# Modulation by two passes with four stationary columns in a one-core hybrid diffusion layer

## Chip, cores and metric

The kernel runs on one core of a Trainium2 chip. The metric is the device time of one execution in microseconds. Before the change three runs took 1698.61, 1699.95 and 1700.68 us; their median is 1699.95 us.

## What is computed

One layer of a diffusion backbone on 1024 latent tokens and 256 context tokens of width 1024. Only its first step matters here: two conditioning vectors, `c` and `c_ctx`, go through silu and a projection, and the first two sixths of the result (shift and scale) modulate the normalised tokens in front of the input projection:

```python
sh1, sc1, gt1, sh2, sc2, gt2 = jnp.split((jax.nn.silu(c) @ w_mod + b_mod)[:, None, :], 6, axis=-1)
sh1c, sc1c, ... = jnp.split(jax.nn.silu(c_ctx) @ w_mod + b_mod, 6, axis=-1)
p = modulate(x, norm1_g, sh1, sc1) @ w_in        # rms_norm(x, g) * (1 + scale) + shift
pc = modulate(xc, norm1_g, sh1c, sc1c) @ w_in
...
```

What follows (differential attention, a gated DeltaNet in both directions, the output projection, sixteen experts chosen by the experts, a final norm) is not touched. All values are float32, w_mod is 1024 x 6144.

## The kernel before

Products of float32 values are made from rounded parts. `K.split(hi, lo, src)` (L174) rounds `src` to fp32r on ACT (L175) and takes the rest, `src - hi`, on DVE or, where it is given, on POOL (L176). `K.mm3` (L167) then multiplies in three passes: high by high (L170), low by high (L171), high by low (L172).

`_modulation` (L525) is the first stage. The small vectors come by seven DMAs into `vr`, 110 rows of 128; PE transposes them (L546), DVE copies them to `vec` (L547). From `vec` come `convw` (L549), half of the two conditioning vectors `xh` (L553), their tanh on ACT (L554) and silu, `cs` (L555). `cs` is split into `csh` and `csl` (L558), for each of eight k-tiles two columns, one for `c` and one for `c_ctx`. These are the stationary operands.

The moving operand is w_mod, columns 0 to 2047, in eight k-tiles `wm` of 128 x 2048 (1 MB each, L532, SP's queue, three buffers). Each k-tile is taken in four parts j of 512 columns: split into `wmh` and `wml` (four buffers each, `WMB`), then multiplied into `pmod`, two rows of PSUM (L574). Of the rests, the one of j = 3 is made on POOL for k-tiles 0 to 5, the others on DVE. In the last k-tile the parts j = 2, 3 are multiplied unsplit, as exact fp32 products (L570). Afterwards the two rows are copied out of PSUM (L581 on ACT, L582 on DVE), turned by sixteen transposes of 2 x 128 (L585), and biases are added (L586, L588): `modA` and `modB`.

Beside this stage the kernel loads the first context tokens and w_in's columns for the values. `K.after` (L115) has POOL write one element of a buffer, so that its load cannot start before a given step. `_tokens` (L593) squares (L603), normalises (L606 to L612) and transposes tokens (L617), and modulates them (L621 to L623); the latent tokens' loads wait for `mod`. `_inproj` (L368) follows: projections of ten token tiles, then of heads. For the rotary heads (L439) halves of the head are exchanged by eight DMAs a half-head from ACT's queue (L449), multiplied on POOL (L452) and written out (L458, L459).

No order is written out by hand. The planner of the tile framework (`schedule_with_timeline_sim=True`, L1743) orders every engine's and every DMA queue's instructions by planned times; of those ready at a time, those of higher priority go first, and `tc.high_priority(n)` raises the priority of what is written under it. On the chip each queue runs strictly in that order, and instructions wait for one another by semaphores.

Of the kernel before, what the change touches and what calls it, by code (L numbers as in the profile page):

```python
# [18 lines left out]
F32 = mybir.dt.float32  # L19
F32R = mybir.dt.float32r  # L20
BF16 = mybir.dt.bfloat16
I32 = mybir.dt.int32
AF = mybir.ActivationFunctionType
ALU = mybir.AluOpType
# [4 lines left out]
P = 128  # L29
D = 1024  # L30
KT = D // P
# [41 lines left out]
QP, WP = (3,), (1, 3, 5)  # L73
# [294 lines left out]
def _inproj(K, banks):  # L368
# [8 lines left out]
    with tc.tile_pool(name="p1v", bufs=1, reuse_waits="tile") as pv, \  # L377
# [3 lines left out]
        with tc.tile_pool(name="p0", bufs=1, reuse_waits="tile") as pe:  # L381
            with tc.tile_pool(name="p0m", bufs=1, space=PSUM, side="right", reuse_waits="tile") as psm:
                xts, *late, raws = _modulation(K, pe, ps0, psm)
            for j in range(4):
                if j < 2:
                    wr = pv.tile([P, 2, 528], F32, name="wvr", bufs=2)
                    K.after(wr[:, 0, 0:1], late[0])
                else:
                    wr = raws.pop(0)[:, :2 * 528].rearrange("p (k f) -> p k f", k=2)
                nc.sync.dma_start(wr[:, :, 0:512], w_in[:, 2 * j:2 * j + 2, 1024:1536])  # L390
                nc.sync.dma_start(wr[:, :, 512:528], w_in[:, 2 * j:2 * j + 2, 3584:3600])
                for i in range(2):
                    K.split(wvh[:, 2 * j + i], wvl[:, 2 * j + i], wr[:, i], nc.gpsimd if 2 * j + i in WP else None)
            K.after(K.cstt[:, 0:1], late[1])
            nc.sync.dma_start(K.cstt, a["cst"][:, P:])
            _tokens(K, pe, ps0, xts, late)
# [119 lines left out]
def _load_tokens(K, pe, t, after=None):  # L516
    xt = pe.tile([P, D], F32, name="xt", bufs=6)
    if after is not None:
        K.after(xt[:, 0:1], after)
    src = K.a["x"][0, t * P:(t + 1) * P] if t < NT else K.a["ctx"][0, (t - NT) * P:(t - NT + 1) * P]  # L520
    K.nc.sync.dma_start(xt, src)
    return xt


def _modulation(K, pe, ps, psm):  # L525

    tc, nc, a = K.tc, K.nc, K.a
    ident = K.cst(C_IDENT)

    def load(kt):  # L530
        wm = pe.tile([P, 2048], F32, name="wm", bufs=3)
        nc.sync.dma_start(wm, a["w_mod"][0, kt * P:(kt + 1) * P, 0:2048])  # L532
        return wm

    vr = pe.tile([110, P], F32, name="vr")
    rows = (a["c"].rearrange("b (k p) -> (b k) p", p=P), a["c_ctx"].rearrange("(k p) -> k p", p=P),
            a["b_mod"].rearrange("l (k p) -> (l k) p", p=P), a["norm1_g"].rearrange("l (k p) -> (l k) p", p=P),
            a["conv_w"].rearrange("l i (k p) -> (l i k) p", p=P), a["gdn_norm_g"], a["da_subln_g"])
    r = 0
    for i, src in enumerate(rows):  # L540
        if i == AT:
            first = load(0)
        (nc.scalar if i % 2 else nc.sync).dma_start(vr[r:r + src.shape[0]], src)
        r += src.shape[0]
    pv = ps.tile([P, 512], F32, name="pv", tag="px", bufs=3)[:, :110]
    nc.tensor.transpose(pv, vr, ident[:110, :110])  # L546
    nc.vector.tensor_copy(K.vec, pv)  # L547
    vec = K.vec
    nc.vector.tensor_scalar(K.convw, vec[:, 72:109], 0.5, None, op0=ALU.mult)  # L549

    xh = pe.tile([P, 16], F32, name="xh")
    th = pe.tile([P, 16], F32, name="th")
    nc.vector.tensor_scalar(xh, vec[:, 0:16], 0.5, None, op0=ALU.mult)  # L553
    nc.scalar.activation(th, xh, AF.Tanh)  # L554
    nc.vector.scalar_tensor_tensor(K.cs, th, 1.0, xh, op0=ALU.add, op1=ALU.mult)  # L555
    csk = K.cs.rearrange("p (w k) -> p k w", w=2)
    csh, csl = (pe.tile([P, KT, 2], F32R, name=nm) for nm in ("csh", "csl"))
    K.split(csh, csl, csk)  # L558
    pm = psm.tile([2, 2048], F32, name="pmod")
    xts, los = {}, []  # L560
    for kt in range(KT):
        wm = load(kt) if kt else first
        if kt in XKT:
            t = TOKENS[XKT.index(kt)]
            xts[t] = _load_tokens(K, pe, t, los[kt - 3])

        for j in (2, 3, 0, 1) if kt == KT - 1 else range(4):
            js = slice(j * 512, (j + 1) * 512)
            if j > 1 and kt == KT - 1:
                nc.tensor.matmul(pm[:, js], csk[:, kt], wm[:, js], start=False, stop=True)  # L570
                continue
            hi, lo = (pe.tile([P, 512], F32R, name=nm, bufs=WMB) for nm in ("wmh", "wml"))
            K.split(hi, lo, wm[:, js], nc.gpsimd if j in QP and kt < 6 else None)
            K.mm3(pm[:, js], csh[:, kt], csl[:, kt], hi, lo, kt == 0, kt == KT - 1)  # L574
        los.append(lo.bitcast(F32)[:, 0:1])
    raws = [pe.tile([P, 2048], F32, name="wvr", tag="wm", bufs=3) for _ in range(2)]
    mrow = pe.tile([P, 2048], F32, name="mrow", tag="wm", bufs=3)[:2]
    mod = pe.tile([P, 8, 2], F32, name="mod")
    with tc.high_priority():
        for i in (1, 0):  # L580
            nc.scalar.activation(mrow[:, i * D:i * D + 512], pm[:, i * D:i * D + 512], AF.Copy)  # L581
            nc.vector.tensor_copy(mrow[:, i * D + 512:(i + 1) * D], pm[:, i * D + 512:(i + 1) * D])  # L582
            pmt = ps.tile([P, 512], F32, name="pmt", tag="px", bufs=3)[:, :16]
            for j in range(8):
                nc.tensor.transpose(pmt[:, 2 * j:2 * j + 2], mrow[:, i * D + j * P:i * D + (j + 1) * P], ident[:2, :2])  # L585
            nc.vector.tensor_tensor(mod if i else K.modB, pmt.rearrange("p (k w) -> p k w", w=2),  # L586
                                    vec[:, 16 + 8 * i:24 + 8 * i].unsqueeze(2).to_broadcast([P, 8, 2]), ALU.add)
        nc.vector.scalar_tensor_tensor(K.modA, mod, 1.0, vec[:, 64:72].unsqueeze(2).to_broadcast([P, 8, 2]),  # L588
                                       op0=ALU.add, op1=ALU.mult)
    return xts, los[LATE[0]], mod[:, 0, 0:1], raws  # L590
# [1156 lines left out]
```

## Time and profile before

| | us |
|---|---|
| median of three runs | 1699.95 |
| the profiled execution | 1699.86 |
| its span, first to last instruction | 1698.1 |
| PE busy | 1540.2 |
| DVE busy | 1301.8 |
| ACT busy | 908.1 |
| POOL busy | 614.3 |

The profiled execution lies 0.09 us under the median, and 1.76 us of it lie around the span. PE, DVE, ACT and POOL are TensorE, VectorE, ScalarE and GpSimd; SP issues DMAs. The busy times are averages over stages of different kinds: the stage that the change touches is the first 42 us or so. In a timeline, a line gives the start, the time taken, the engine, the line of the kernel and the tiles; consecutive instructions of one kind are drawn together (x4), and what stands in brackets is the engine's idle time just before and what ended it. A matmul's duration is longer than its distance from the next one, since they are pipelined.

### The profile page before, as it was taken

The page shows a single profiled execution, that of the slowest core. Times are in us where ns is not written, and L with a number is a line of the kernel's source. Part 1 is how long each engine was busy: PE and PEld are TensorE (multiplying, and loading weights), DVE is VectorE, ACT ScalarE, POOL GpSimd, SP SyncE. Part 2 cuts the span into 40 slices and gives each one's busy share as a digit, 9 for nine tenths or more (in the row PEclk, how much of TensorE's full clock was granted, in tenths as well). Part 3 has the DMA queues.
Part 4 walks back from the last instruction along what each step waited for, and adds up shares of the span by engine and source line. Part 5 has one row for each costly group of instructions (what it writes and reads, how often), then busy time and mean ns, then how long its engine had stood idle before and what let it go on. Part 6 is the DMA issues. An engine that isn't in the chain of part 4 may idle for free.

```text
span 1698.1 us, 24820 instructions
## 1 busy us (share of the span) xinstructions
PE 1540.2 (91%) x8782; PEld 1301.7 (77%) x8782; DVE 1301.8 (77%) x2111; ACT 908.1 (53%) x1508; POOL 614.3 (36%) x554
## 2 busy tenths in 40 slices
PE   6999889899988999999898898399999999999994
PEld 2897668788867988888888787278888887778882
DVE  6657654586768877778787644799999998899986
ACT  6521125344423655656565232288777776777772
POOL 3013331322236774482720122435355433342101
PEclk9999999999997999999999999599999999999997
DMA  7477943444556042413122584699999999999965
GB/s 271 164 246 223 282 137 118 142 124 130 181 162 173 20 111 78 120 64 108 58 86 86 159 294 169 243 361 343 403 396 395 379 397 377 355 387 386 363 245 185
DMA packets 171280, 378.76 MB, mean 223 GB/s; under 512 B 32590, under 2 KB 82188, under 8 KB 170004
## 3 DMA queue, kind: packets, MB, share of 16 engines
q1 hardware_dynamic: 131874, 315.22, 51.2%
q0 software_dynamic: 12096, 45.09, 8.9%
q10 hardware_dynamic: 27186, 16.86, 3.8%
q8 instruction: 69, 1.13, 0.3%
q14 instruction: 55, 0.45, 0.1%
HBM read 316.65 MB, written 56.29 MB: 220 GB/s over the span
## 4 chain that ended last, share of the span: by engine, by line
PE 54%; DVE 14%; DMA 7%; POOL 3%; issue 3%; ACT 3%; SPq 1%; ACTq 0%; POOLq 0%; DVEq 0%
PE pgu L170 4%; PE pgu L172 3%; PE pgu L171 3%; PE pgv L172 3%; PE pgv L170 3%; PE pgv L171 3%; PE py L170 3%; PE py L171 3%; PE py L172 3%; PE po L1066 2%; DMA qe<-eg_dram 2%; PE sp L1038 2%; PE pp L170 2%; PE pp L171 2%; PE sp L1039 2%
## 5 line engine op out<-in xcount | busy, mean ns | idle before, releaser
L1478 DVE TENSOR_TENSOR wlo<-raw,whi 128x1024 fp32r<-128x1024 f32 x368 | 439.4, 1238 | 29.7 <-ACT whi L1477 10.0
L1477 ACT ACTIVATE whi<-raw 128x1024 fp32r<-128x1024 f32 x376 | 390.8, 1060 | 102.5 <-PE pgu L171 36.4
L1425 POOL TENSOR_SCALAR onehot<-fcst,slot 128x128 bf16<-128x128 f32 x96 | 142.0, 1493 | 156.9 <-PE pls L1428 156.9
L171 PE MATMUL pl<-XH,wl 128*128 128x512 f32 x384 | 152.8, 398 | 3.6 <-DVE wl L176 3.6
L170 PE MATMUL pl<-XH,wh 128*128 128x512 f32 x384 | 153.1, 399 | 0.9 <-DVE ab L411 0.9
L172 PE MATMUL pl<-XL,wh 128*128 128x512 f32 x384 | 153.4, 399 | 0.0
L1044 ACT ACTIVATE pt<-sp,mx 128x1280 f32<-128x1280 f32 x64 | 84.9, 1326 | 56.7 <-DVE mx L1041 56.1
L1041 DVE TENSOR_REDUCE mx<-sp 128x1 f32<-128x1280 f32 x64 | 95.0, 1485 | 22.1 <-PE sp L1039 22.0
L170 PE MATMUL pgu<-whi,xTh 128*128 128x512 f32 x256 | 102.2, 399 | 5.0 <-ACT xTh L175 4.2
L172 PE MATMUL pgu<-wlo,xTh 128*128 128x512 f32 x256 | 101.7, 397 | 0.0
L172 PE MATMUL pgv<-wlo,xTh 128*128 128x512 f32 x256 | 101.2, 395 | 0.0
L171 PE MATMUL pgu<-whi,xTl 128*128 128x512 f32 x256 | 100.9, 394 | 0.0
L170 PE MATMUL pgv<-whi,xTh 128*128 128x512 f32 x256 | 100.6, 393 | 0.0
L171 PE MATMUL pgv<-whi,xTl 128*128 128x512 f32 x256 | 100.2, 391 | 0.0
L170 PE MATMUL py<-whi,hTh 128*128 128x512 f32 x240 | 94.6, 394 | 2.0 <-DVE y L1542 2.0
L172 PE MATMUL py<-wlo,hTh 128*128 128x512 f32 x240 | 94.6, 394 | 0.9 <-DVE wlo L1478 0.9
L171 PE MATMUL py<-whi,hTl 128*128 128x512 f32 x240 | 95.0, 396 | 0.0
L170 PEld LDWEIGHTS pl<-XH,wh 128*128 128x128 f32 x384 | 73.4, 191 | 20.4 <-issue 5.2
L171 PEld LDWEIGHTS pl<-XH,wl 128*128 128x128 f32 x384 | 73.2, 191 | 20.1 <-DVE wl L176 3.9
L1066 PE MATMUL po<-V,aT 128*128 128x128 f32 x640 | 87.8, 275 | 0.0
L1038 PE MATMUL sp<-KH,QS 128*128 128x512 f32 (+1 forms) x192 | 77.0, 401 | 9.9 <-ACT pt L1044 5.7
L172 PEld LDWEIGHTS pl<-XL,wh 128*128 128x128 f32 x384 | 73.2, 191 | 15.4 <-issue 0.9
(560 smaller groups left out, 3995.9 us busy)
## 6 DMA issues: line engine op xcount, KB each, us to landing
raw<-w_gate SPq DMA_DIRECT2D x64, 1024.0 KB
raw<-w_up SPq DMA_DIRECT2D x64, 1024.0 KB
raw<-w_down SPq DMA_DIRECT2D x64, 1024.0 KB
rwm<-w_mod POOLq DMA_DIRECT2D x32, 512.0 KB, 6.3
wr<-w_in ACTq DMA_DIRECT2D x24, 512.0 KB
wm<-w_mod SPq DMA_DIRECT2D x8, 1024.0 KB
KH<-qk_dram SPq DMA_DIRECT2D x16, 320.0 KB
xt<-x SPq DMA_DIRECT2D x8, 512.0 KB
```

The source lines that it names most:

```text
L170: nc.tensor.matmul(out, ah, bh, start=start, stop=False)
L171: nc.tensor.matmul(out, al, bh, start=False, stop=False)
L172: nc.tensor.matmul(out, ah, bl, start=False, stop=stop)
L1038: nc.tensor.matmul(sp[:, k0:k1], qs, st["KH"][s][:, k0:k1], start=True, stop=False)
L1039: nc.tensor.matmul(sp[:, k0:k1], padded[t % 2][:, s], st["KL"][:, k0:k1], start=False, stop=True)
L1041: nc.vector.tensor_reduce(mx, sp[:, :LT], axis=AX.X, op=ALU.max, negate=True)
L1044: nc.scalar.activation(pt, sp[:, :LT], AF.Exp, bias=mx, accum_out=sm)
L1066: nc.tensor.matmul(po, aT[c], st["V"][:, c], start=c == 0, stop=c == NTT - 1)
L1425: eng.tensor_scalar(oh[:, t], iota, slot[:, t, e:e + 1], None, op0=ALU.is_equal)
L1477: nc.scalar.activation(hi, raw[:, i], AF.Copy)
L1478: eng.tensor_tensor(lo, raw[:, i], hi.bitcast(F32), ALU.subtract)
```

## The change

- The rounded parts and the rests of silu lie side by side in one tile `cs4`: for each k-tile four columns, rounded `c`, rounded `c_ctx`, rest of `c`, rest of `c_ctx`. One pass with `wmh` and one with `wml` as the moving operand give four rows of PSUM; the product of the two rests comes in as well. The three-pass `mm3` is not used here any more.
- The four rows are summed while they are turned: instead of a transpose, a product with `both`, a 4 x 2 tile with ones where row and row + 2 are to be added.
- The chain from `vr` to `cs4` stands under a priority of 5000, and `convw` behind it.
- For j = 0, 1 of the first k-tile the rounding goes from ACT to POOL (a copy), and the rest is made on DVE as before.

```diff
@@ -542,21 +542,25 @@
-    pv = ps.tile([P, 512], F32, name="pv", tag="px", bufs=3)[:, :110]
-    nc.tensor.transpose(pv, vr, ident[:110, :110])
-    nc.vector.tensor_copy(K.vec, pv)
     vec = K.vec
-    nc.vector.tensor_scalar(K.convw, vec[:, 72:109], 0.5, None, op0=ALU.mult)
 
     xh = pe.tile([P, 16], F32, name="xh")
     th = pe.tile([P, 16], F32, name="th")
-    nc.vector.tensor_scalar(xh, vec[:, 0:16], 0.5, None, op0=ALU.mult)
-    nc.scalar.activation(th, xh, AF.Tanh)
-    nc.vector.scalar_tensor_tensor(K.cs, th, 1.0, xh, op0=ALU.add, op1=ALU.mult)
     csk = K.cs.rearrange("p (w k) -> p k w", w=2)
-    csh, csl = (pe.tile([P, KT, 2], F32R, name=nm) for nm in ("csh", "csl"))
-    K.split(csh, csl, csk)
-    pm = psm.tile([2, 2048], F32, name="pmod")
+    cs4 = pe.tile([P, KT, 4], F32R, name="cs4")
+    with tc.high_priority(5000):
+        pv = ps.tile([P, 512], F32, name="pv", tag="px", bufs=3)[:, :110]
+        nc.tensor.transpose(pv, vr, ident[:110, :110])
+        nc.vector.tensor_copy(vec, pv)
+        nc.vector.tensor_scalar(xh, vec[:, 0:16], 0.5, None, op0=ALU.mult)
+        nc.scalar.activation(th, xh, AF.Tanh)
+        nc.vector.scalar_tensor_tensor(K.cs, th, 1.0, xh, op0=ALU.add, op1=ALU.mult)
+        K.split(cs4[:, :, 0:2], cs4[:, :, 2:4], csk)
+    nc.vector.tensor_scalar(K.convw, vec[:, 72:109], 0.5, None, op0=ALU.mult)
+
+    both = pe.tile([4, 2], F32, name="both")
+    nc.vector.tensor_tensor(both, ident[:4, 0:2], ident[:4, 2:4], ALU.add)
+    pm = psm.tile([4, 2048], F32, name="pmod")
     xts, los = {}, []
     for kt in range(KT):
@@ -567,14 +571,20 @@
         for j in (2, 3, 0, 1) if kt == KT - 1 else range(4):
             js = slice(j * 512, (j + 1) * 512)
             if j > 1 and kt == KT - 1:
-                nc.tensor.matmul(pm[:, js], csk[:, kt], wm[:, js], start=False, stop=True)
+                nc.tensor.matmul(pm[:2, js], csk[:, kt], wm[:, js], start=False, stop=True)
                 continue
             hi, lo = (pe.tile([P, 512], F32R, name=nm, bufs=WMB) for nm in ("wmh", "wml"))
-            K.split(hi, lo, wm[:, js], nc.gpsimd if j in QP and kt < 6 else None)
-            K.mm3(pm[:, js], csh[:, kt], csl[:, kt], hi, lo, kt == 0, kt == KT - 1)
+            if not kt and j < 2:
+
+                nc.gpsimd.tensor_copy(hi, wm[:, js])
+                nc.vector.tensor_tensor(lo, wm[:, js], hi.bitcast(F32), ALU.subtract)
+            else:
+                K.split(hi, lo, wm[:, js], nc.gpsimd if j in QP and kt < 6 else None)
+            nc.tensor.matmul(pm[:, js], cs4[:, kt], hi, start=kt == 0, stop=False)
+            nc.tensor.matmul(pm[:, js], cs4[:, kt], lo, start=False, stop=kt == KT - 1)
         los.append(lo.bitcast(F32)[:, 0:1])
     raws = [pe.tile([P, 2048], F32, name="wvr", tag="wm", bufs=3) for _ in range(2)]
-    mrow = pe.tile([P, 2048], F32, name="mrow", tag="wm", bufs=3)[:2]
+    mrow = pe.tile([P, 2048], F32, name="mrow", tag="wm", bufs=3)[:4]
     mod = pe.tile([P, 8, 2], F32, name="mod")
@@ -582,7 +592,7 @@
             for j in range(8):
-                nc.tensor.transpose(pmt[:, 2 * j:2 * j + 2], mrow[:, i * D + j * P:i * D + (j + 1) * P], ident[:2, :2])
+                nc.tensor.matmul(pmt[:, 2 * j:2 * j + 2], mrow[:, i * D + j * P:i * D + (j + 1) * P], both, start=True, stop=True)
```

## Rows read from the trace of the kernel before

**Rows 1.** Page, part 2: PE's busy tenths in 40 slices.
```profile
PE   6999889899988999999898898399999999999994
```

**Rows 2.** Windows: us, busy us (x instructions) by engine, PEclk, DMA share, GB/s.
```profile
16.30:19.70 3.40, 3.40 (x17) 1.23 (x15) 2.68 (x4) 3.27 (x7) 1.83 (x2) 1.00 0.30 53
19.70:33.90 14.20, 11.62 (x49) 3.31 (x47) 11.81 (x22) 11.57 (x21) 6.76 (x6) 1.00 1.00 396
33.90:42.30 8.40, 7.46 (x39) 2.86 (x37) 8.30 (x13) 5.91 (x11) 4.25 (x5) 1.00 0.37 93
42.30:49.40 7.10, 5.52 (x25) 4.66 (x24) 4.66 (x10) 3.76 (x7) 2.23 (x5) 0.52 0.98 354
...
25.00:30.00 5.00, 3.29 (x13) 0.76 (x11) 4.66 (x13) 3.17 (x7) 2.98 (x3) 1.00 0.99 380
```

**Rows 3.** Timeline of ACT, 0 to 46 us: start, us, what, [idle before <-releaser].
```profile
6.83 2.19 ACT L175 ACTIVATE wmh<-wm 128x512 fp32r<-128x512 f32 x4 [3.17 <-DMA wm<-w_mod]
...
10.74 0.22 ACT L175 ACTIVATE csh<-cs 128x16 fp32r<-128x16 f32 x1 [1.61 <-DVE cs L555]
13.40 0.63 ACT L175 ACTIVATE wmh<-wm 128x512 fp32r<-128x512 f32 x1 [2.44 <-PE pmod L171]
...
26.53 2.19 ACT L175 ACTIVATE wmh<-wm 128x512 fp32r<-128x512 f32 x4 [0.55 <-PE pmod L172]
30.12 2.19 ACT L612 ACTIVATE xt<-xt,nt 128x1024 f32<-128x1024 f32 x2 [1.40 <-DVE nt L163]
...
36.43 1.13 ACT L175 ACTIVATE wmh<-wm 128x512 fp32r<-128x512 f32 x2
```

**Rows 4.** Timeline of PE, 10 to 16 us.
```profile
11.01 1.87 PE L170 MATMUL pmod<-wmh,csh 128*2 128x512 f32 x4 [3.74 <-ACT csh L175]
12.68 0.63 PE L171 MATMUL pmod<-wmh,csl 128*2 128x512 f32 x1
...
15.24 0.40 PE L171 MATMUL pmod<-wmh,csl 128*2 128x512 f32 x1
15.48 0.40 PE L172 MATMUL pmod<-wml,csh 128*2 128x512 f32 x1
```

**Rows 5.** Timeline of SP's queue: the issue of k-tile 4.
```profile
17.83 0.33 SPq L532 DMA_DIRECT2D wm<-w_mod  x1
```

**Rows 6.** Timeline of DVE, 0 to 46 us.
```profile
7.31 0.27 DVE L547 COPY vec<-pv 128x110 f32<-128x110 f32 x1 [7.31 <-PE pv L546]
7.50 0.69 DVE L176 TENSOR_TENSOR wml<-wm,wmh 128x512 fp32r<-128x512 f32 x1
...
8.20 0.17 DVE L553 TENSOR_SCALAR xh<-vec 128x16 f32<-128x16 f32 x1
...
9.48 1.23 DVE L555 SCALAR_TENSOR_TENSOR cs<-th,xh 128x16 f32<-128x16 f32 x1
...
42.92 0.55 DVE L622 TENSOR_SCALAR xm<-px,modA,modB 128x256 f32<-128x256 f32 x1 [0.63 <-ACT XH L621]
```

**Rows 7.** Timeline of POOL, 0 to 46 us.
```profile
9.11 1.57 POOL L176 TENSOR_TENSOR wml<-wm,wmh 128x512 fp32r<-128x512 f32 x1 [8.68 <-ACT wmh L175]
...
42.56 1.31 POOL L176 TENSOR_TENSOR wvl<-wvr,wvh 128x528 fp32r<-128x528 f32 x1
```

**Rows 8.** Groups of POOL, by form: the copy nearest in size.
```profile
L343 POOL COPY fb<-cst 80x512 f32<-80x512 f32 x4 | 2.5, 614 | 0.0
```

**Rows 9.** Timeline of PE from 35 us: the exact products, the result's transposes.
```profile
35.81 1.88 PE L570 MATMUL pmod<-wm,cs 128*2 128x512 f32 x4
...
40.70 0.66 PE L585 MATMUL pmt<-ident,mrow 2*128 2x2 f32 x8
...
41.65 0.40 PE L585 MATMUL pmt<-ident,mrow 2*128 2x2 f32 x4
```

**Rows 10.** Chain that ended last, 200 to 260 us: start, us, what.
```profile
246.00 0.61 ACTq L449
...
249.49 3.28 POOL rxs L452
```

## Prediction, written before the changed kernel was run

> **What bounds the kernel now.** I read the page's slices first, then the windows of the first 60 us, then each engine's timeline there. After its first slice TensorE (PE) is busy in tenths of 8 and 9 through most of the run [rows 1], so a microsecond saved in front, while PE still waits for the modulation, should arrive at the end. The change touches nothing behind about 42.3 us directly; what it can save is looked for ahead of that.
>
> There the windows show three things [rows 2]. DMA, the source of the eight 1 MB k-tiles of w_mod, is saturated from 19.70 to 33.90 us (share 1.00, 396 GB/s), but in the 3.40 us before that it stands almost still (0.30, 53 GB/s). In the last 8.40 us the DVE is the engine that is full (8.30 us). PE is not full in 19.70 to 33.90 (11.62 of 14.20 us): its count of passes is not in itself the limit.
>
> The hole in the DMA has a cause that can be followed back. There are three buffers for k-tiles; k-tile 4 is issued at 17.83 us [rows 5], once every part of k-tile 1 has been split. ACT began to split k-tile 1 only at 13.40 us, after 2.44 us of waiting for PE's pass L171 [rows 3]: the four buffers of rounded parts were still being read. And PE began only at 11.01 us, when ACT had made csh [rows 3, 4]. So the bound is a latency: vector chain, then PE, then ACT, then the DMA's ring.
>
> **Start of PE.** Removed from the path to csh: convw, and DVE and ACT work planned ahead of the chain (ACT does four splits from 6.83 us for 2.19 us, two of which go to POOL). Without any hold: vec ends at 7.58; five short steps (xh 0.17, then tanh, cs, rounded part 0.22 and rest at the same 0.17 to 0.22) make 0.95 us, and hand-overs with ACT, which is busy until 6.83 + 2.19/2 = 7.9 us with its two remaining splits, some 0.3 us more: 8.8 us [rows 3, 6]. That is the early end.
>
> But two copies are added on POOL at just this time. Near copies took 0.61 us each [rows 8]. The row of cs shows what they can do: 1.23 us for 16 columns, when xh took 0.17; it ends at 10.71, just after POOL's subtraction ended at 9.11 + 1.57 = 10.68 [rows 6, 7]. The DVE stood still for POOL. An operation that reads PSUM was not held: xm took 0.55 us inside POOL's 1.31 us [rows 6, 7]; so vec should pass, xh may not. I take one hold by a copy, 0.61 us, and one subtraction wml put between, 0.69 us [rows 6]: PE starts at 8.8 + 1.3 = 10.1 us. Late end: cs is held by POOL's subtraction again, 1.23 - 0.17 = 1.06 us more: 11.2 us.
>
> The Trainium skill (SBUF — State Buffer, Who interferes with whom) speaks against this part: the engine that issues first keeps the pair of ports shared by VectorE and GpSimd for its whole instruction, and the other blocks. By that rule xh, cs and the rest could each be held in turn, and the sum would come out at its late end, a gain of under 1 us. The cs row agrees; whether all three are held no row here shows.
>
> **Two passes instead of three.** 30 products lose a pass: 90 passes become 60. At the spacing after 15.24 us, 0.24 us (the spacing before it was (12.68 - 11.01)/4 = 0.42 us) [rows 4], that is 7.2 us of PE work. I cost most of this at nothing: in 19.70 to 33.90 us DMA, ACT and DVE cover it [rows 2]. What counts is the first k-tile. Before, the buffer of j=0 became free only when the pass with csl had read it, 13.40 - 11.01 = 2.39 us behind PE's start. Now one product with four columns reads it: from the start of that last reading pass to ACT's next split it was 13.40 - 12.68 = 0.72 us [rows 3, 4]. So k-tile 1 begins at 10.1 + 0.72 = 10.8 us instead of 13.40: **2.6 us earlier** (bounds: 8.8 + 0.72 = 9.5, or 3.9 earlier; 11.2 + 0.72 = 11.9, or 1.5 earlier). The pace after that is unchanged until PE is at its full clock: two passes a product then as now.
>
> **How it carries.** k-tile 4 is issued 2.6 us earlier, at 15.2 us; the hole shrinks from 3.4 to 0.8 us, and all later landings move by 2.6 us. One further wait of ACT for PE, 0.55 us at 26.53, should go too, since a k-tile now has 8 passes in place of 12 [rows 3]. The DVE's work in the last 8.4 us is unchanged, so it moves along. Together 3.1 us (3.9 + 0.55 = 4.5 at most, 1.5 at least).
>
> **What is added.** The last transposes become full fp32 products with `both`. Two exact fp32 products left four records of PE, while 8 transposes left 8 records in 0.66 us and 4 in 0.40 us [rows 9]; so the added products leave twice the records, at (0.66 - 0.40)/4 = 0.065 us each. The last four cost 0.26 us on the path, the eight before them up to 0.52 us more; they wait for the copies out of PSUM, so I take 0.5 in all (0.26 to 0.78). The tile `both` is made from ident while DVE waits for its first operand until 7.31 us [rows 6]: nothing; without that cover one short step, 0.17 us. The copies of four rows instead of two have the same columns: nothing. The two copies on POOL delay its subtraction of k-tile 0 by nothing where ACT's fourth split ended at 6.83 + 2.19 = 9.02, since two copies end at 8.1; with that cover gone they delay the ring's next issue by at most 1.2 us, about what separates the late start from the one I take. cs4 takes the room of csh and csl. No DMA is added.
>
> **The sum** is 3.1 - 0.5 = 2.6 us off the profiled execution's 1699.86 us (span 1698.1 and 1.76 around it; the median of the runs is 1699.95, the same to 0.1): **1697.3 us**. Bounds: 4.5 - 0.26 = 4.2 and 1.5 - 0.78 = 0.7 us gained, 1695.7 to 1699.2. A measurement of this kernel can tell about 0.2%, 3.4 us, from no change.
>
> **Rivals.** *More than the latency.* If nothing holds the chain (3.9) and ACT's 1.40 us wait at 30.12 for the context tokens' norm [rows 3] also goes with a less crowded DVE: 3.9 + 0.55 + 1.40 - 0.5 = 5.3 us, 1694.5. For it: ACT and DVE have such idle spots all along. Against: DVE is at 11.81 of 14.20 us and DMA at 1.00 [rows 2], and neither has less to do. In 42.30 to 49.40 us the clock was granted at 0.52 on average [rows 2], near the 1.2 GHz level; if the shift lets PE run that stretch at 2.4 GHz, its 5.52 busy us shrink by up to 2 us: 1692.5.
>
> *The chain is not ahead.* If POOL's copies and subtraction hold it as before, PE starts at 11.2 us, and only the earlier release is left: 1.5 - 0.5 = 1 us, 1699.
>
> *PE falls to half its clock.* With a third fewer passes PE has gaps between k-tiles. At 0.42 us a pass, 60 passes from 10.1 us end at 35.3, the exact products at twice 1.88 us at 39.1; the transposes begin then rather than at 40.70, and take 1.0 us more: 0.6 us gained, 1699.3, no change. Against it: in 25 to 30 us PE was busy 3.29 of 5 us and the clock stayed at 1.00 [rows 2], and 8 passes at 0.24 us in the 2.65 us that 1.05 MB takes at 396 GB/s are about the same share. The Trainium skill (TensorE: Matmul & The Clock Gate, HAM oscillation — how this bites in real kernels) warns of this pattern, bursts of matmuls between waits for the next tile; by that rule this rival would be the likeliest, and the 25 to 30 us row disagrees.
>
> *Slower: another plan for a queue far behind.* All queues are ordered by a planner from planned times, which move as well. The stage at 200 to 260 us is on the chain that ended last through ACT's queue of rope exchanges, 0.61 us an issue, eight for a half-head, and then POOL's product of 3.28 us [rows 10]. If the new plan puts one half-head's issues in front of those that are waited for, that is 8 x 0.61 + 3.28 = 8.2 us; less 2.6, slower by 5.6: 1705.5. It decides from 2.6 us of added wait on; one burst without the product is +2.3, 1702.2. For it: these queues run in order, and each issue is long. Against: a uniform shift leaves the order as it is.
>
> **Chances.** Forecast 0.42, of which 0.12 beyond 3.4 us (bound 4.2); more than the latency 0.30; not ahead 0.06; half clock 0.06; slower plan 0.16. Faster by over 0.2%: 0.12 + 0.30 = 0.42. Within: 0.30 + 0.06 + 0.06 = 0.42. Slower: 0.16. The range goes from the clock's 1692.5 to one burst with the late start, 1699.86 - 0.7 + 4.9 = 1704.
>
> **What would show it.** Right: PE's first product near 10.1 us, ACT's split of k-tile 1 near 10.8, the issue of k-tile 4 near 15.2, a hole in the DMA of under 1.5 us, no wait of ACT for PE behind 20 us, the first XH near 39.7 us, and the same offset at 240 us and at the end. Wrong: PE's start at or behind 11 us with xh, cs or the rest drawn out beside a POOL copy; a granted clock of 0.5 between 16 and 38 us; or an offset at 240 us unlike that at 40 us, which would be the planner's.

## The result, and the profile after

The changed kernel took 1706.68 us (median of 8 runs, 1704.40 to 1712.49), the kernel before, in the same session, 1698.26 us (8 runs, 1691.96 to 1701.89). The ratio is 1.0058, 95% interval 1.0040 to 1.0075: the change makes it slower by 0.6%, where 2.6 us less had been forecast. The profiled execution took 1704.40 us, its span is 1702.6 us, so again 1.8 us lie around it.

The chain that the prediction followed did what it said. On PE, ACT and SP, in timelines of the changed kernel (from the copies of `mrow` on, line numbers are ten above those of before):

```profile
9.85 0.59 PE L583 MATMUL pmod<-wmh,cs 128*4 128x512 f32 x1 [2.41 <-DVE cs L176]
...
26.59 0.40 PE L584 MATMUL pmod<-wml,cs 128*4 128x512 f32 x1 [1.40 <-DVE wml L176]
...
28.34 0.39 PE L584 MATMUL pmod<-wml,cs 128*4 128x512 f32 x1 [1.12 <-DVE wml L176]
...
38.34 0.40 PE L584 MATMUL pmod<-wml,cs 128*4 128x512 f32 x1
39.41 2.84 PE L595 MATMUL pmt<-both,mrow 4*128 4x2 f32 x24 [0.68 <-ACT mrow L591]
...
42.55 1.48 PE L595 MATMUL pmt<-both,mrow 4*128 4x2 f32 x8
```

```profile
10.47 0.63 ACT L175 ACTIVATE wmh<-wm 128x512 fp32r<-128x512 f32 x1 [0.98 <-PE pmod L583]
...
24.10 2.20 ACT L175 ACTIVATE wmh<-wm 128x512 fp32r<-128x512 f32 x4 [0.51 <-DMA wm<-w_mod]
28.39 2.19 ACT L622 ACTIVATE xt<-xt,nt 128x1024 f32<-128x1024 f32 x2 [2.09 <-DVE nt L163]
...
38.77 0.59 ACT L591 ACTIVATE mrow<-pmod 4x512 f32<-4x512 f32 x1 [2.94 <-PE pmod L584]
40.10 0.59 ACT L591 ACTIVATE mrow<-pmod 4x512 f32<-4x512 f32 x1 [0.74 <-DVE mrow L592]
...
45.37 1.48 ACT L631 ACTIVATE XH<-px,modB,modA 128x256 fp32r<-128x256 f32 x3 [1.85 <-DVE modB L596]
```

```profile
15.25 0.33 SPq L532 DMA_DIRECT2D wm<-w_mod  x1
...
24.32 0.45 SPq L532 DMA_DIRECT2D wm<-w_mod  x1
```

Of the kernel before, the last k-tile's issue, the last product into `pmod`, the last add of the modulation and the first XH:

```profile
27.37 0.34 SPq L532 DMA_DIRECT2D wm<-w_mod  x1
...
40.16 0.39 PE L172 MATMUL pmod<-wml,csh 128*2 128x512 f32 x1
...
42.12 0.17 DVE L586 TENSOR_TENSOR modB<-pmt,vec 128x16 f32<-128x16 f32 x1
...
42.32 0.56 ACT L621 ACTIVATE XH<-px,modB,modA 128x256 fp32r<-128x256 f32 x1 [0.43 <-DVE modB L586]
```

Against these and [rows 3 to 5]: PE starts at 9.85 us instead of 11.01, ACT splits k-tile 1 at 10.47 instead of 13.40, k-tile 4 is issued at 15.25 instead of 17.83. The last k-tile's issue moved from 27.37 to 24.32 us, 3.05 earlier. But at 28.39 us, where ACT normalises the context tokens, the lead is 1.73 us (30.12 in [rows 3]); at the last product into `pmod` it is still 1.8 (38.34 + 0.40 = 38.74, against 40.16 + 0.39 = 40.55). From there on everything is later: XH starts at 45.37 us instead of 42.32.

These are single executions, and some of these times scatter. Two more profiles of the front of before (e17 and e3 below) end the last product at 39.27 and 41.59 us, two more of the changed front (e1 and e2) at 38.48 and 38.60. Over three profiles each, the mean lead is 3.4 us at the last issue and 1.9 us at the last product. What follows the last product does not scatter: from its end to the start of `modB` it is 1.56 or 1.57 us in all three profiles of the old front and 6.44 or 6.45 us in all three of the new one. DVE, and POOL's one row, show this end in detail:

```profile
7.87 1.29 DVE L559 TENSOR_SCALAR convw<-vec 128x37 f32<-128x37 f32 x1
9.08 0.16 DVE L557 SCALAR_TENSOR_TENSOR cs<-th,xh 128x16 f32<-128x16 f32 x1
...
39.39 0.68 DVE L592 COPY mrow<-pmod 4x512 f32<-4x512 f32 x1 [1.11 <-ACT mrow L591]
40.72 0.68 DVE L592 COPY mrow<-pmod 4x512 f32<-4x512 f32 x1 [0.65 <-ACT mrow L591]
...
43.03 2.23 DVE L176 TENSOR_TENSOR wvl<-wvr,wvh 128x528 fp32r<-128x528 f32 x2 [0.61 <-ACT wvh L175]
45.18 0.16 DVE L596 TENSOR_TENSOR modB<-pmt,vec 128x16 f32<-128x16 f32 x1
```

```profile
7.86 1.26 POOL L176 TENSOR_TENSOR wml<-wm,wmh 128x512 fp32r<-128x512 f32 x1
```

Three things stand between 38.74 and 45.18 us. The four copies out of `pmod` go one behind the other, each waiting for the one before on the other engine (39.39, 40.10 and 40.72 us). The products with `both` follow at (2.84 - 0.25)/23 = 0.11 us a record, two records a product; the last eight, where the clock falls, take 1.48. And when they are done, at 42.55 + 1.48 = 44.03 us, DVE is not free: the planner has put two splits of the next matrix ahead of `modB`, 43.03 to 45.2 us.

The first two of these rows of DVE belong together with POOL's. `convw` takes 1.29 us where it took 0.18 before, beside POOL's subtraction, and `cs`, whose tanh is ready at 8.21 us, starts only behind it, at 9.08. In e1, the same kernel once more, `convw` starts 0.02 us ahead of POOL's subtraction (7.88 to 9.16 us) instead of 0.01 us behind it; it takes 0.18 us, and `cs` itself is drawn out, to nearly the same end:

```profile
7.86 0.18 DVE L559 TENSOR_SCALAR convw<-vec 128x37 f32<-128x37 f32 x1
8.23 0.95 DVE L557 SCALAR_TENSOR_TENSOR cs<-th,xh 128x16 f32<-128x16 f32 x1 [0.20 <-ACT th L556]
```

The windows, as in [rows 2], and PE's slices, as in [rows 1]:

```profile
16.30:19.70 3.40, 3.04 (x13) 0.74 (x12) 2.96 (x5) 3.40 (x8) 1.29 (x1) 1.00 1.01 416
19.70:33.90 14.20, 9.31 (x27) 1.60 (x26) 10.37 (x23) 11.30 (x20) 5.39 (x6) 0.84 0.85 329
33.90:42.30 8.40, 7.72 (x36) 3.56 (x35) 6.55 (x9) 4.17 (x8) 3.90 (x4) 0.86 0.48 132
42.30:49.40 7.10, 6.35 (x29) 5.17 (x30) 4.98 (x10) 3.75 (x8) 2.44 (x6) 0.55 0.91 334
```

```profile
PE   6999889899977999999998898299999999999994
```

The hole in the DMA is gone (share 1.01 instead of 0.30). The granted clock is 0.84 and 0.86 from 19.70 to 42.30 us, where it was 1.00: it stays at 1.00 until 29.2 us and is 0.58 from there to 37.3 us, behind two waits of PE for DVE (1.40 us at 26.59, 1.12 us at 28.34). In the slices PE falls from 8 to 7 in the twelfth and thirteenth, 468 to 553 us.

Far behind, at 520 to 1000 us, the views differ too. What the change touches ends at 45 us, but the planner put other instructions first there on all engines; from some 80 to 520 us and behind 1000 us the order is nearly the same. PE's waits from 520 to 1000 us (total us, times, longest), of the kernel before and of the changed one:

```profile
PE sp L1038 <- ACT pt L1044: 5.7, 8, 1.9
```

```profile
PE sp L1048 <- ACT pt L1054: 11.1, 9, 2.9
PE pot L1092 <- DVE aO L1089: 6.8, 2, 6.5
```

The wait for `aO`, one of 6.5 us, is not there before. The same wait stands in all four profiles that have the new order behind 520 us (this one and, of the runs below, e1, e3 and e16) and in none of the fifteen with the old one.

### The profile page after: what moved, and what is told of

It is laid out like the page before. It is cut to its first block, busy times and chain, and to the rows that moved or that the text cites. A ratio compares the mean times of both kernels' runs of the same rounds, so it can differ in the third digit from the quotient of the medians.

```text
span 1702.6 us, 24783 instructions
## 1 busy us (share of the span) xinstructions
PE 1538.4 (90%) x8768; PEld 1299.5 (76%) x8768; DVE 1309.3 (77%) x2112; ACT 906.9 (53%) x1506; POOL 612.3 (36%) x556
## 4 chain that ended last, share of the span: by engine, by line
PE 57%; DVE 11%; DMA 6%; ACT 3%; POOL 3%; issue 3%; SPq 0%; ACTq 0%; POOLq 0%; DVEq 0%
PE pgu L170 4%; PE pgu L172 3%; PE pgu L171 3%; PE pgv L171 3%; PE pgv L170 3%; PE pgv L172 3%; PE py L172 3%; PE py L170 3%; PE py L171 3%; PE po L1076 2%; DMA qe<-eg_dram 2%; PE pl L172 2%; PE pl L170 2%; PE pl L171 2%; PE sp L1048 2%
```

## The experiments

The runs e1 to e17 have five rounds each, 12 executions of the kernel beside 17 to 35 of the kernel before on the same chip; the groups below ran on different chips, so runs are compared by their ratios. Single executions of one kernel scatter by 4 us (standard deviation; the kernel before went from 1691.5 to 1709.5 us), so a ratio is known to 0.002 and single profiles say less than the medians. Two more numbers of each profile are worked out by matching its instructions, by line, tile and count, with those of the first profile of before: the **offset**, the median difference of starts from 85 to 110 us, in the projections; and the **stretch**, what the offset gains from 480 to 495 us to 1000 to 1040 us.

| run | XH starts | offset | stretch | ratio, 95% interval |
|---|---|---|---|---|
| before, first profile | 42.3 | 0 | 0 | 1 |
| changed, first profile | 45.4 | 1.6 | +4.2 | 1.0058, 1.0040 to 1.0075 |
| e1 changed again | 45.1 | 0.9 | +2.8 | 1.0062, 1.0043 to 1.0082 |
| e2 new front, old order behind | 45.2 | 2.8 | -0.3 | 1.0041, 1.0020 to 1.0062 |
| e3 old front, new order behind | 43.4 | 0.9 | +0.8 | 1.0030, 1.0010 to 1.0050 |
| e4 e2 with transposes | 43.6 | 1.2 | -3.7 | 1.0009, 0.9989 to 1.0029 |
| e5 e4 with quarters | 43.7 | 3.4 | -5.4 | 1.0028, 1.0009 to 1.0046 |
| e6 e2 with quarters | 46.7 | 1.9 | +0.7 | 1.0040, 1.0023 to 1.0056 |
| e7 chain first, three passes | 41.9 | 0.3 | -5.4 | 0.9994, 0.9973 to 1.0016 |
| e8 e5, chain not first | 44.2 | 3.3 | -1.8 | 1.0016, 0.9994 to 1.0038 |
| e9 e5, order held | 42.6 | 0.2 | -5.0 | 1.0003, 0.9983 to 1.0023 |
| e10 e2, order held | 45.6 | 2.3 | -2.6 | 1.0037, 1.0018 to 1.0056 |
| e11 e9, third pass of zeros | 43.2 | 0.1 | -0.7 | 0.9997, 0.9980 to 1.0015 |
| e12 e4, order held | 44.0 | 1.0 | -6.4 | 0.9993, 0.9975 to 1.0012 |
| e13 e9, transposes four times | 46.4 | 4.6 | -7.0 | 1.0028, 1.0006 to 1.0050 |
| e14 e10 again | 46.1 | 2.1 | -0.3 | 1.0013, 0.9990 to 1.0036 |
| e15 e9 with idle products | 45.8 | 2.6 | +1.3 | 1.0004, 0.9985 to 1.0023 |
| e16 e9, new order behind | 42.3 | -0.1 | +1.0 | 1.0041, 1.0023 to 1.0059 |
| e17 before, order held | 41.0 | -0.4 | -2.4 | 0.9997, 0.9973 to 1.0021 |

The front of e3 and of e17 is that of before, in its order too, and XH starts there at 43.4 and 41.0 us: differences of 1 us in the column of XH are within what executions differ by.

### Front or order behind: e1 to e4

An order is held by dependences without a semaphore (`info`) between neighbours of one engine's list (cut):

```diff
+        for i, j in zip(seq, seq[1:]):
...
+            tc.add_manual_dep(traced[j], traced[i].name, info, reason="issue order")
```

e1 is the changed kernel. e2 is the changed kernel with before's lists from 520 us on, e3 the kernel before with the changed kernel's lists from there on. e4 is e2 with transposes of four rows, and a second add on DVE in place of the sum in `both` (the index of `mrow` and the lines between are cut):

```diff
-                nc.tensor.matmul(pmt[:, 2 * j:2 * j + 2], mrow[...], both, start=True, stop=True)
+                nc.tensor.transpose(pmt[:, 4 * j:4 * j + 4], mrow[...], ident[:4, :4])
...
+            nc.vector.tensor_tensor(to, p4[:, :, 2:4], to, ALU.add)
```

> The changed kernel once more, so that the others have it beside them on one chip. Both theories: 4 to 9 us slower than the kernel before (ratio 1.002 to 1.006), with XH of the first tokens near 45.4 us against 42.3, and an offset at 490 us of +0.5 to +1.5 us against the kernel before's trace.

> The changed kernel, with every engine's and queue's order from the heads' preparation on (about 520 us to the end) pinned to the order of the kernel before. Theory A, the new plan behind 520 us costs most: within 2 us of the kernel before (about +0.6, the offset at 490 us), and clearly faster than the changed kernel. Theory B, the later end of the modulation is what costs: the same as the changed kernel, +4 to +9 us.

> The kernel before, with the order from about 520 us on pinned to that of the changed kernel. Theory A: 4 to 8 us slower than the kernel before. Theory B: the same as the kernel before, within 2 us.

> The changed kernel with the order behind 520 us pinned to that of before, and the eight products with the 4 x 2 tile of ones put back to transposes (of four rows), the two pairs of rows being added on DVE. Theory A with the products as the front's fault: modB 2.5 to 4 us earlier than in the changed kernel (41 to 42.5 us), the total 0 to 3 us faster than the same kernel with the products. Rival: the half clock between 29 and 37 us is the front's fault, and modB comes no more than 1 us earlier.

Both halves cost: 1.0041 for the front alone, 1.0030 for the order alone, 1.0062 together. In e4 the transposes take most of the front's part away; e5 and e8, which have them too, stand at 1.0028 and 1.0016.

### What in the front: e5 to e8

In e5 and e6 each quarter of `pmod` and of `mrow` is a tile of its own; else a copy of four rows out of one tile waited for the copies beside it (1.11, 0.74 and 0.65 us above). The quarters of `mrow` also take the splits' buffers instead of a k-tile's:

```diff
-    pm = psm.tile([4, 2048], F32, name="pmod")
+    pms = [psm.tile([4, 512], F32, name="pmod%d" % j) for j in range(4)]
```

e5 has transposes, e6 the products. e7 is the kernel before (three passes, its own end) with the chain under its priority and POOL's two copies. e8 is e5 without these two ("the first run of this group" is e5).

> The changed kernel with transposes of four rows (and two adds on DVE) in place of the products with both, with the order of the kernel before behind 520 us, and now with the four quarters of pmod and of mrow as tiles of their own, so that the four copies of mrow wait for the products of their own quarter alone, not for one another. Theory S (the copies that went one behind the other, 38.77, 39.39, 40.10 and 40.72 us in the changed kernel, ate what the chain had gained): the copies of the second half start before the last splits' products, modB comes at 40 to 41.5 us (42.12 before, 42.49 in the last run of this form), the first XH near 41.5, and the time is 0.999 of before (0.997 to 1.000). Rival R (the end of the front does not set the time; the planned order or the spread behind it does): modB comes early all the same, but the ratio stays at 1.001 (1.000 to 1.003).

> The same quarters, but with the products with both kept, as the change has them; order of the kernel before behind 520 us. Theory S: the copies part from one another, worth some 1.9 us of the 3.05 by which XH came late; the sixteen products still take 0.22 us each, 0.16 more than a transpose, so that modB comes near 43 us and the ratio falls from 1.0041 to 1.002 (1.001 to 1.003). Rival B (the products with both alone cost the time): it stays at 1.004 (1.003 to 1.005).

> The kernel before, with three passes and its own copies and transposes, and the chain to the rounded parts of silu(c) set first as the change sets it (with the first two rests' copies on POOL), order of the kernel before behind 520 us. Theory S and the prediction's first step: PE starts near 9.9 us, ACT splits k-tile 1 near 10.5 to 11, the hole of the DMA is gone, and what was gained stays, since nothing at the end of the modulation is changed: modB near 40 us, ratio 0.9985 (0.997 to 0.9995). Rival (more reaches the end than that gain or nothing does, since the stage behind has its own bound): 1.000 (0.9993 to 1.001).

> The form of the first run of this group with the chain left at its old priority and without the copies on POOL: two passes of four columns alone, order of the kernel before behind 520 us. Theory S: PE starts near 11 us as before, the DMA keeps its hole of some 3 us, and PE's third less work is worth the wait of 0.55 us at 26 us at most: modB at 41 to 42.5, ratio 1.000 (0.999 to 1.001). Rival (the two passes themselves cost, since PE then falls to half its clock in the modulation): granted clock under 0.9 in 19.7 to 42 us, ratio 1.002 or more.

The copies came apart (e5: ACT's at 38.0 and 39.8 us), but theory S fell: e5 and e6 are no faster than e4 and e2. Their orders show why `modB` was no earlier: the planner had filled the freed time with splits of the next matrix, so that e5's second add of `modB` came at 43.42 us with its transposes done at 41.95. e8 decides nothing: the clock is at 0.80 and 0.73, as its rival asks, and the ratio, 1.0016, lies between the two theories. e7 is the test of the prediction's first step. ACT in e7:

```profile
41.91 0.57 ACT L626 ACTIVATE XH<-px,modB,modA 128x256 fp32r<-128x256 f32 x1 [0.74 <-DVE modB L591]
43.81 1.18 ACT L175 ACTIVATE wvh<-wvr 128x528 fp32r<-128x528 f32 x2 [1.34 <-DMA wvr<-w_in]
```

PE starts at 9.51 us, 1.50 earlier, and k-tile 4 is issued at 16.68, 1.15 earlier; 0.4 us of that is left at XH, less than the front of before scatters by, and the next split waits for the DMA of w_in in both kernels (43.81 us; before 43.95). The ratio is 0.9994, nothing that can be told from no change. That a lead at PE's start reaches the end, the prediction's first premise, is not shown by it.

### The order of the front held: e9 to e12

Now every list behind the modulation is that of before from its first instruction on, `modB` ahead of the two splits, XH ahead of ACT's later splits and of the squares of the next tokens. e9 has quarters and transposes; e10 is the changed front as it is; e12 is e9 with one tile each again. e11 adds to e9 a third product, with four columns of zeros, `z4`:

```diff
+            nc.tensor.matmul(pms[j], z4, hi, start=False, stop=False)
```

> Two passes with four columns, the chain first, quarters of pmod and mrow as tiles of their own, transposes with two adds; and now every engine's order behind the modulation is that of the kernel before from the first instruction on, with DVE's end of the modulation as there too: modB's adds ahead of the second and third split of the third matrix group, XH ahead of ACT's later splits and of the squares. Theory O (the planner's filling of the end of the modulation with splits and squares is what the front costs): modB at 40.5 to 41.7 us, first XH by 42, the offset of the projections at 85 to 110 us against the kernel before under 1 us (1.2 to 3.4 in the four runs of this form so far), ratio 0.9995 (0.998 to 1.001). Rival H (half the clock in the modulation, which two passes bring, costs it): offset of 1 us or more all the same, ratio 1.002 (1.001 to 1.004).

> The changed kernel's front as it is (products with both, one tile of pmod and of mrow, copies one behind the other), with the order of the kernel before on every engine behind the modulation and at its end, as in the run ahead of this. Theory O: most of the 7 us that this front cost with its own order is gone; what is left are the copies that wait for one another (1.9 us) and the products with both, so modB near 43.5 us, offset at 85 to 110 us of 1 to 2, ratio 1.001 (1.000 to 1.0025). Rival B (copies and products at the end cost it, whatever the order): ratio 1.004 (1.003 to 1.005).

> The first run of this group with a third product for each rounded part, against four columns of zeros (it adds nothing to the sums): PE has the work of three passes again. Rival H: the granted clock is 1.00 from 16 to 42 us (0.75 to 0.84 with two passes), and the time falls against the first run of this group by 0.002. Theory O: the clock may well be 1.00, but PE was not what ended last, so the two agree within 0.001.

> The first run of this group with one tile of pmod and one of mrow again: the copies wait for one another, all else as there. Tells what that wait costs by itself once the order is held: by the starts of the copies (38.77 to 40.72 in the changed kernel, 37.47 to 40.59 before) 0.5 to 1.9 us at modB; ratio higher than the first run's by 0.0003 to 0.001 by theory O, by none if the end of the front has slack.

With transposes and the order held nothing of the front's cost is left: 1.0003, 0.9997, 0.9993. In e12 the copies that wait for one another put the second add of `modB` at 43.72 us, in e9 at 42.37, and the ratio does not show it. In e11 the granted clock went up from 0.82 to 0.99 in 19.70 to 33.90 us (not behind that: 0.89 and 0.82), and the time stayed. The third product changes more than the clock: k-tile 4 is issued at 16.83 us, in e9 at 15.78. First e9, then e11:

```profile
19.70:33.90 14.20, 8.61 (x24) 1.60 (x24) 9.66 (x21) 9.99 (x18) 4.96 (x5) 0.82 1.01 391
33.90:42.30 8.40, 7.40 (x34) 2.62 (x32) 8.28 (x14) 5.66 (x11) 4.18 (x5) 0.89 0.26 73
```

```profile
19.70:33.90 14.20, 10.68 (x42) 2.82 (x41) 9.85 (x23) 10.43 (x18) 6.21 (x6) 0.99 1.02 406
33.90:42.30 8.40, 8.40 (x38) 2.99 (x36) 7.70 (x13) 5.67 (x11) 3.63 (x4) 0.82 0.29 74
```

e10 keeps the products, and is at 1.0037, against theory O and as rival B has it. Its PE and DVE, where DVE now stands ready 2.64 us ahead of `modB`:

```profile
39.75 3.19 PE L595 MATMUL pmt<-both,mrow 4*128 4x2 f32 x24 [0.68 <-ACT mrow L591]
43.49 1.86 PE L595 MATMUL pmt<-both,mrow 4*128 4x2 f32 x8
```

```profile
45.39 0.17 DVE L596 TENSOR_TENSOR modB<-pmt,vec 128x16 f32<-128x16 f32 x1 [2.64 <-PE pmt L595]
```

The last eight records take 1.86 us, 0.22 each, at half the clock (0.50 granted in 42.30 to 49.40 us); four transposes took 0.40 [rows 9].

The time from the end of the last product into `pmod` to the last add of `modB` can now be taken apart. It is 1.6 us before, 2.0 with transposes, quarters and a second add (e9, e11), 3.6 with one tile (e12), and 6.3 and 5.5 with one tile and the products (e10, and e14 below); in the changed kernel, with its own order, it is 6.4. So the copies that wait take 1.6 us of it, the products 1.9 to 2.7, the order of the end up to 1.0.

### Lateness, products or chance; the order once more: e13 to e17

e13 writes each transpose of e9 four times. e14 is e10 again. e15 is e9 with sixteen products with `both` whose results nothing uses. e16 is e9 with the changed kernel's lists from 520 us on. e17 is the kernel before with its own lists written out.

> Run e9's kernel (1.0003 of before, offset 0.16 us at 85 to 110 us) with each of the sixteen transposes of the end written four times: 48 more records of 0.065 us, some 3.1 us at full clock, between the copies and modB, and no product with both. Theory L (what the front costs is lateness of modB and nothing else, and behind 110 us it grows): modB at 44.5 to 46 us, offset at 85 to 110 us of 1.8 to 2.8, ratio 1.0035 (1.002 to 1.005) as with the products. Theory P (lateness of 2 us costs 2 us; what the changed front costs above that hangs on the products with both): ratio 1.001 (1.000 to 1.002).

> Run e10's kernel once more, beside the others of this group: products with both, copies one behind the other, order held. Both theories: 1.0037 again (1.002 to 1.0055), offset at 85 to 110 us near 2.3; a ratio under 1.002 would say that run e10 stood high by chance.

> Run e9's kernel with sixteen products with both whose results nothing uses (four rows of the vectors against both, four ahead of each of k-tiles 3 to 6), where PE has idle time. Theory L: no lateness, so no cost, 1.000 (0.999 to 1.001), modB within 0.5 us of 42.2. Theory P: the products themselves cost wherever they stand, 1.003 (1.002 to 1.0045).

> Run e9's kernel with the order of the changed kernel from 520 us on in place of that of the kernel before. The theory that this order costs by itself (run e3: 1.0030): 1.003 (1.0015 to 1.0045), and the stretch from 495 to 1000 us longer by 3 to 7 us than in e9's profile, whatever the front. Rival (it cost by chance of what stood before it): 1.000 to 1.001.

> The kernel before with its own order written out by the means that held the order in the runs e2 to e16; the instructions and their order on each engine are those of the kernel before. All theories: 1.000 (0.999 to 1.001). Its profile is a second execution of the kernel before: what it differs by from the first in the stretches 85 to 495, 495 to 1000 and 1000 us to the end is what single profiles differ by from one execution to the next; if it lies 3 to 8 us above the first one at 495 us, as thirteen of the other sixteen profiles do, the first profile was a low one there, and nothing of that stretch is put down to any front.

e14, the same kernel as e10, gives 1.0013. By what was expected, that says that e10 stood high by chance; the two together give 1.0025.

e13 makes `modB` late without any of the products (45.91 us), and costs what they cost, 1.0028. e15 missed its aim: the planner moved all sixteen products ahead, fourteen of them to the very start, where they stood in front of the first product into `pmod` (13.55 us, in e9 9.89), the last two to 15.35 and 16.38 us. Its PE:

```profile
7.49 6.13 PE L570 MATMUL idle<-both,vr 4*128 4x2 f32 x28
13.55 1.02 PE L587 MATMUL pmod<-wmh,cs 128*4 128x512 f32 x2
```

So it became one more kernel with `modB` late, at 45.28 us, and late from PE's start on, and yet it took 1.0004. Theory P, the products as such, has no support left: e13 costs without them, e15 has them and shows no cost. Theory L is right in the mean only. Taken together, with the order held, XH at 42.6 to 44.0 us (e9, e11, e12) gives 0.9998 on average and XH at 45.6 to 46.4 (e10, e13, e14, e15) gives 1.0020: 3.8 us for 2.7 us of lateness, with single runs between 0.7 and 6.3. That lateness grows on its way is not shown. That it counts rests on this mean; e15 alone shows none, and what sets it apart from e13 no run tells.

e16 confirms the order's part on another front: 1.0041 against e9's 1.0003. PE's waits in e16 have the same row as the changed kernel's:

```profile
PE pot L1092 <- DVE aO L1089: 6.7, 2, 6.4
```

The stretch from 495 to 1000 us grew in all four profiles with the new order (+0.8 to +4.2, mean 2.2) and has a mean of -2.6 in the fifteen with the old one, of which one (e15) lies above +0.8: 4.8 us apart. The pairs of times say the same: 0.0030 (e3), 0.0038 (e16 less e9), 0.0021 (e1 less e2), on average 5 us. e17, whose order is written out by the same means and takes 0.9997, shows no cost of holding an order by itself.

e17, with the same instructions as before, differs from the first profile by +1.8 us from 85 to 495 us and by -2.4 us from 495 to 1000: so much at least do two executions differ by. No front is blamed for the stretch of 85 to 495 us.

## Why the prediction was wrong

**The start of PE, the release, the ring: right, the first in part by luck.** PE at 9.85 us (10.1 forecast), k-tile 1 at 10.47 (10.8), k-tile 4's issue at 15.25 (15.2), no hole, the wait of 0.55 us gone (24.10 us waits for DMA), the last k-tile issued 3.05 us earlier (3.1). But the 1.3 us of holds in that sum were not those that came. Neither POOL's copies (0.61) nor a subtraction `wml` put between (0.69) held the chain. POOL's subtraction did, which had been priced for the late end alone: it kept `cs` waiting for 0.8 us, in this profile through `convw`, which still stood ahead of `cs` on DVE, in e1 directly. That the late end did not come is because the other 1.3 us were not there. The Trainium skill (SBUF — State Buffer, Who interferes with whom) says that of the two engines the one that issues first holds the shared ports for its whole instruction, and the other blocks; these rows agree.

**"The DVE's work in the last 8.4 us is unchanged, so it moves along": wrong by 1.3 us.** The issue led by 3.05 us, the last product by 1.8 (in the means of three profiles 3.4 and 1.9). What did not move along is the context tokens' norm, on which ACT waits (2.09 us at 28.39, 1.40 before): ACT's next splits stand behind it, and the lead is 1.73 us from there on. Its rows were at hand; it was named only as something that a rival might gain.

**"I take 0.5 in all" for what is added: wrong, and the largest error in the front.** From the last product into `pmod` to `modB` it was 1.6 us (40.55 to 42.12) and became 6.4 (38.74 to 45.18): 4.9 us more, where 0.5 was priced. Mis-sized were the products: a record was priced at a transpose's spacing, 0.065 us, and measured 0.11, at half the clock 0.22; they took 1.9 to 2.7 us. Left out altogether were the copies, "the same columns: nothing", which now wait for one another (1.6 us), and the planner, which put splits ahead of `modB` (up to 1.0 us). The first XH came 3.05 us later instead of 2.6 earlier. By the mean of e10 and e13 to e15 a lateness of that size is worth about 0.002; the front with its own order costs 0.004 (e2, e6).

**"A uniform shift leaves the order as it is": wrong; the slower rival was right in kind, wrong in place.** It had a new plan for a queue far behind, at 200 to 260 us, for 8.2 us, and gave 0.16 to it. The new plan came at 520 to 1000 us, on every engine, for 5 us (e3, e16), with a new wait of 6.5 us for `aO`. The argument against it, the uniform shift, failed: the order did change there, on every engine. That the planner goes by its own times, in which the edit need not be a uniform shift, is the likely reason; no run tests it. The forecast offset "the same at 240 us and at the end" could not be read from one pair of profiles at all (e17).

**Half the clock: it came for part of the way, and no cost of it can be measured.** The granted clock was 0.84 in 19.70 to 33.90 us, and 0.58 from 29.2 to 37.3. The Trainium skill (TensorE: Matmul & The Clock Gate, HAM oscillation — how this bites in real kernels) warns of bursts of matmuls between waits for the next tile. The trace agrees, and the row of 25 to 30 us of before, which the prediction trusted instead, was the wrong witness. But PE itself waited for DVE in that stretch (1.40 and 1.12 us), and e11 against e9 (0.9997 and 1.0003, each known to 0.002) shows no gain from 0.99 instead of 0.82, though e11 changes more than the clock. Only at the end, where in e10 PE alone stands before `modB`, does the low clock show: 0.22 instead of 0.11 us a record for the last eight, some 0.9 us (8 x 0.11).

The parts add up within their errors: about 0.003 for the order behind, 0.002 for the late `modB` and 0.0015 to 0.0025 for the front's own order (e2, e6 against e10, e14; e4, e5, e8 against e9, e11, e12), each known to about 0.002, against 0.0058 and 0.0062 measured. Shown best is the order behind: three pairs agree, and its wait for `aO` stands in the four profiles that have it and in no other. Open is where behind 110 us the front's part grows from the 2 us that the offset shows.

No version beats the kernel before: the best ones, e7, e9, e11 and e12, lie within 0.9993 and 1.0003. Two passes instead of three save PE's time in a stretch in which PE waits for others.

## What to carry to other kernels

Price the end of a stage as carefully as its start: a lead gained at the head of a chain passes through every shared step on its way (here a norm, then copies, small products and one add), and the last few small instructions stand on the path alone. Where a planner orders the queues, a small edit is two changes, its own and a new order of everything behind it; hold the order of before to tell them apart, and look at the instructions just ahead of the late one on its engine. Judge such sizes by many executions: two profiles of the same instructions differed by 2 us in a stretch of 500 us, and by 1.3 us at XH in the first 42.

## What was not expected of the hardware

An exact product of a 4 x 128 operand with a 4 x 2 one leaves two records 0.11 us apart, 0.22 us in all, and a transpose of two or four rows one of 0.065: the smaller product is the dearer one.

Which of two short instructions of DVE is drawn out beside POOL's subtraction hangs on some 0.01 us. In the five profiles in which `convw` starts 0.01 to 0.02 us behind the subtraction (the changed kernel's first, e12, e14, e15, e16) it takes 1.28 to 1.30 us. In nine others with the chain first it starts 0.01 to 0.11 us ahead (e1, e2, e4 to e7, e9, e10, e13); there it takes 0.17 to 0.18, and `cs`, which starts next, takes 0.95 to 1.03 instead of 0.16.

The granted clock of one stretch differs between executions. Here are 400 to 420 us of before and of e17, the same instructions 1.9 us later:

```profile
400.00:420.00 20.00, 20.00 (x94) 16.55 (x94) 18.96 (x53) 8.61 (x26) 2.87 (x2) 1.00 0.32 89
```

```profile
400.00:420.00 20.00, 20.00 (x87) 16.37 (x87) 17.75 (x50) 8.73 (x26) 2.00 (x2) 0.93 0.28 81
```

That it makes the spread of the times is not shown: e14 has 1.00 there too, and is 8.7 us behind.
